# Start addresses of TensorE's operands at multiples of 256 bytes, and activations stored with all high parts ahead of all low parts

## The chip, the cores and the metric

The kernel runs on one core of a Trainium2 chip. The metric is the device time of one execution in microseconds (us), and a kernel's time is the median over its runs.

## The reference, cut to what matters

One layer of an encoder trunk on 256 tokens of width 1024, all in fp32:

```
x = x + 1/2 * SwiGLU_1(RMSNorm(x))                 # 1024 -> 2 x 2816 -> 1024
h = RMSNorm(x);  u = h @ W_in                      # 1024 -> 7904, split into parts
a = MLA(parts of u)                                # 16 heads of 96, 256 x 256 scores
m = BiSSD(parts of u)                              # conv, 32 heads, two scans, 2 chunks of 128
x = x + W_out( sigmoid(gA) * (a @ P_A) + sigmoid(gB) * (m @ P_B) )
x = x + 1/2 * SwiGLU_2(RMSNorm(x))
```

The weights are 124.5 MB, read once.

## The kernel before, in words

Activations lie transposed in SBUF: 128 features on the partitions (a "k tile"), 256 tokens along the free dimension. The weights stream through: `wload` (L112) fetches a piece of up to 1088 columns by one DMA on SP's queue, ScalarE writes its high part `whi` in the type fp32r, VectorE writes the rest `wlo = raw - whi`, and there are four buffers of each (raw, whi, wlo). An activation is split in the same way (`split`, L127) into a high part xh and a low part xl.

A product is three terms: whi·xh + whi·xl + wlo·xh. TensorE holds a 128 x 128 block of a weight still ("stationary", loaded by its own LDWEIGHTS ahead of each matmul) and streams 256 or 512 columns of the activation ("moving"). There are two forms of it:

- `wstat` (L135): three matmuls of 256 columns for each k tile, at L141, L142 and L143, into one accumulator. It serves W_in (`ps_in`), the second half of P_B (`ps_sb`), P_A (`ps_ab`) and W_out (`ps_o`, where the left operand is xs).
- `wstat2` (L145): a pair for each k tile, a matmul of 512 columns at L154 (whi against xh and xl, which lie side by side) and one of 256 at L153 (wlo against xh; the first of a chain is L156). It serves gate and up (`ps_gu`), down (`ps_d`), the gates gA and gB, and the first half of P_B (both `ps_half`).

The moving tiles are `xs` ([128, k, 2, 256]: for each k tile the high part and behind it the low part; two buffers in turn), `hs` (the hidden layer of 22 k tiles) and `ms` (the scan's output of 8 k tiles). In the attention's own projection (`ps_qkv`, L563 to L570) the roles are swapped: the weight moves, 192 or 256 columns, and a block of `cqh`, `cql`, `ckh` or `ckl` is stationary. Scores, transposes and the scan's last product are plain fp32 matmuls (`ps_sc`, `ps_pT`, `ps_xT`, `ps_cb`, `ps_y`).

The stages in order of time: gate and up of the first FFN (to 137 us of the span), down (to 200), W_in's first columns and first group (to 240), then attention heads, scan groups and the remaining columns of W_in interleaved by a table of keys (to 540), P_A, P_B and W_out (to 616), gate and up (to 733) and down of the second FFN. Within a stage the code's order sets each engine's order.

Where a tile starts in SBUF follows from the order in which pools are opened: one group grows from low addresses (`const`, `raw`, `w`, `x`, `xn`, `small`, then the stage's own pools), one from the high end (`pre` for W_in's first pieces, `ssd` for the scan). Addresses are per partition, in bytes; all are multiples of 32. What matters of them is the remainder by 256:

| tile | role on TensorE | start mod 256 before | after |
|---|---|---|---|
| whi, wlo (four buffers each) | stationary (moving in ps_qkv) | 32 | 0 |
| whi, wlo in pool pre | stationary in the first ps_in | 224 | 192 |
| xs (both buffers) | moving | 32 | 0 |
| hs | moving | 160 | 0 |
| ms | moving | 64 | 0 |
| cqh, cql, ckh, ckl | stationary | 160 | 0 |
| msk4 / eye / st1 | moving / stationary / moving (ps_pl) | 32 / 32 / 64 | 160 / 160 / 160 |
| cst (identity) | moving in transposes, fp32 | 0 | 128 |
| xz, xd, E | fp32 operands of the scan | 224 | 192 |
| qk, kv, pr | fp32 operands of attention | 192, 64, 64 | 32, 160, 160 |

A k tile, a block of a weight and a buffer are each a multiple of 256 bytes long, so a tile's remainder holds for all its slices.

Of the kernel before, what the change touches and what calls it, by code (L numbers as in the profile page):

```python
# [8 lines left out]
F32 = mybir.dt.float32  # L9
F32R = mybir.dt.float32r  # L10
# [5 lines left out]
P = 128  # L16
# [7 lines left out]

RAWB, WB = 4, 4
NMM, NPL, NG = 3, 2, 3
EB, PRB, QKB = 4, 2, 2
# [45 lines left out]
def build(ctx, tc, A, out, dbg=None):  # L73
# [6 lines left out]

    cp = ctx.enter_context(pool("const"))
    rawp = ctx.enter_context(pool("raw", RAWB))
    wp = ctx.enter_context(pool("w", WB))
    xp = ctx.enter_context(pool("x"))
    xnp = ctx.enter_context(pool("xn", 2))
    sm = ctx.enter_context(pool("small", 2))

    def dump(name, ap):
# [46 lines left out]
    def wstat(ps, pieces, xs, k0, first, last):  # L135

        ks = [(pc, j) for pc, j0, n in pieces for j in range(j0, j0 + n)]
        for i, (pc, j) in enumerate(ks):
            w = slice(j * P, (j + 1) * P)
            xh, xl = xs[:, k0 + i, 0], xs[:, k0 + i, 1]  # L140
            TE.matmul(ps, pc.hi[:, w], xh, start=first and i == 0, stop=False)  # L141
            TE.matmul(ps, pc.hi[:, w], xl, start=False, stop=False)  # L142
            TE.matmul(ps, pc.lo[:, w], xh, start=False, stop=last and i == len(ks) - 1)  # L143

    def wstat2(ps, pieces, xs, k0, first, last):  # L145


        ks = [(pc, j) for pc, j0, n in pieces for j in range(j0, j0 + n)]
        for i, (pc, j) in enumerate(ks):
            w = slice(j * P, (j + 1) * P)  # L150
            a, b = first and i == 0, last and i == len(ks) - 1
            if not a:
                TE.matmul(ps[:, 0], pc.lo[:, w], xs[:, k0 + i, 0], start=False, stop=False)  # L153
            TE.matmul(ps, pc.hi[:, w], xs[:, k0 + i], start=a, stop=b)  # L154
            if a:
                TE.matmul(ps[:, 0], pc.lo[:, w], xs[:, k0 + i, 0], start=False, stop=False)  # L156

# [53 lines left out]
    def xn_tiles():  # L211
        return xnp.tile([P, KD, 2, T], F32R, tag="xs", name="xs")

    class Norm:
# [12 lines left out]
        def scale(self, k):  # L227
            g = vec[:, self.vcol + k:self.vcol + k + 1]
            split(self.xs[:, k, 0], self.xs[:, k, 1], x[:, k], g)

# [15 lines left out]
    def ffn(norm, wgu, wd, after, hook=None):  # L246
        with ExitStack() as es:
# [3 lines left out]
            ps_r = es.enter_context(pool("ps_fr", 2, space=PSUM, reuse_waits="tile"))  # L251
            hs = hp.tile([P, KF, 2, T], F32R, name="hs")
            R = None
            for f in range(KF):
# [22 lines left out]
                tt(sg, sg, gu[:, 1], ALU.mult)  # L277
                split(hs[:, f, 0], hs[:, f, 1], sg)
            for d in range(KD):
# [97 lines left out]
    with ExitStack() as es:  # L377
# [9 lines left out]


        cqh = mp.tile([P, 3, T], F32R, name="cqh")
        cql = mp.tile([P, 3, T], F32R, name="cql")  # L390
# [18 lines left out]
        for k in range(KD):  # L409
            xr = m0.tile([P, T], F32, tag="xr", name="xr", bufs=2)  # L410
            stt(xr, x[:, k], vec[:, V_MIX + k:V_MIX + k + 1], R, ALU.mult, ALU.mult)
            split(xs[:, k, 0], xs[:, k, 1], xr)

# [93 lines left out]
        as_ = xn_tiles()  # L507
        ms = mp.tile([P, 8, 2, T], F32R, name="ms")
        mpb = mp.tile([P, 8, T], F32, name="mpb")

# [38 lines left out]
        def attn_group(g):  # L549
# [53 lines left out]
            def head(h):  # L603
# [31 lines left out]
                if h % 2:  # L635
# [7 lines left out]
                    i = g * HG // 2 + h // 2  # L643
                    split(as_[:, i, 0], as_[:, i, 1], po[:, :T])

# [3 lines left out]
        def ssd_group(g, xz):  # L649
# [57 lines left out]
            def finish():  # L707
# [10 lines left out]
                o = 4 * (g % 2)  # L718
                split(ms[:, o:o + 4, 0], ms[:, o:o + 4, 1], y)
                dump(f"m{g}", y)  # L720
# [63 lines left out]
        for c in range(4):  # L784
            branch(1, c)
            for d in range(2 * c, 2 * c + 2):
                tmp = mpb[:, d]
                tt(tmp, tmp, gt[4 + d // 2][:, d % 2], ALU.mult)
                tt(tmp, tmp, gt[d // 2][:, d % 2], ALU.add)
                split(os_[:, d, 0], os_[:, d, 1], tmp)  # L790
        dump("mg", mpb)
# [113 lines left out]
```

## Time and profile before

| | us |
|---|---|
| median of 3 runs | 811.11 |
| lowest, highest | 809.4, 811.33 |
| the profiled execution | 809.85 |
| its span, first to last instruction | 808.1 |
| TensorE busy in the span | 786.8 |
| VectorE, ScalarE busy | 625.0, 493.6 |

A matmul's row in the trace lasts from its start to the end of its results, and the next one starts while it still drains. So the busy time of TensorE counts drains too, and what a matmul costs in a row of them is the distance from its start to the next one's start, not its duration.

### The profile page before, as it was taken

Reading aid. Unit: us, or ns where it says so; the run is one execution under the profiler, and the core shown is the slowest. Engines: PE = TensorE matmul, PEld = TensorE weight load, DVE = VectorE, ACT = ScalarE, POOL = GpSimd, SP = SyncE. Lnnn points to the kernel's source line nnn. Section 1 sums busy time; section 2 is a strip of 40 time slices with the busy share of each in tenths; the row PEclk is TensorE's granted clock in tenths of the full one; section 3 lists DMA queues with packets and bytes.
Section 4 is the critical chain, followed back from the end, with each engine's and each line's share of the span. In section 5 each row is a group of like instructions: output and inputs, shape, how many; then the busy total and the mean of one; then the engine's idle time right before and its main releaser. Section 6 shows DMA issues by size and latency. Waiting matters only on the chain.

```text
span 808.1 us, 13739 instructions
## 1 busy us (share of the span) xinstructions
PE 786.8 (97%) x5232; PEld 700.4 (87%) x5232; DVE 625.0 (77%) x1276; ACT 493.6 (61%) x866; POOL 0.2 (0%) x4
## 2 busy tenths in 40 slices
PE   5999999999998999999999999999999999999998
PEld 4888888888998998988988887888998888888887
DVE  5899987667797986897898678767787877777553
ACT  6667665555367659569667675567455655655442
POOL 0000000000000000000000000000000000000000
PEclk9999999999999999999999999999999999999999
DMA  7667774667134443322325514441755465564772
GB/s 262 207 196 241 237 237 145 180 187 233 40 104 162 132 135 103 108 79 89 100 82 159 176 54 146 137 135 56 232 172 191 161 204 181 189 188 138 197 211 75
DMA packets 39090, 126.46 MB, mean 156 GB/s; under 512 B 4464, under 2 KB 5872, under 8 KB 39024
## 3 DMA queue, kind: packets, MB, share of 16 engines
q1 hardware_dynamic: 38592, 124.69, 48.6%
q10 hardware_dynamic: 432, 0.89, 0.3%
q8 instruction: 41, 0.67, 0.3%
q14 instruction: 25, 0.20, 0.1%
HBM read 124.52 MB, written 1.05 MB: 155 GB/s over the span
## 4 chain that ended last, share of the span: by engine, by line
PE 87%; DVE 6%; ACT 5%; issue 1%; DMA 1%; ACTq 0%
PE ps_gu L154 20%; PE ps_d L154 10%; PE ps_gu L153 9%; PE ps_half L154 5%; PE ps_d L153 5%; PE ps_in L142 4%; PE ps_in L143 4%; PE ps_in L141 4%; PE ps_y L700 3%; PE ps_half L153 2%; PE ps_sc L613 2%; PE ps_o L640 1%; PE ps_gu L156 1%; PE ps_pl L682 1%; DVE wlo L97 1%; PE ps_pT L630 1%
## 5 line engine op out<-in xcount | busy, mean ns | idle before, releaser
L97 DVE TENSOR_TENSOR wlo<-raw,whi 128x1024 fp32r<-128x1024 f32 (+4 forms) x256 | 289.1, 1131 | 75.5 <-ACT whi L94 74.6
L94 ACT ACTIVATE whi<-raw 128x1024 fp32r<-128x1024 f32 (+4 forms) x256 | 251.6, 986 | 145.4 <-PE ps_d L154 51.2
L154 PE MATMUL ps_gu<-xs,whi 128*128 128x512 f32 x704 | 243.8, 400 | 7.8 <-DVE xs L100 7.7
L153 PE MATMUL ps_gu<-xs,wlo 128*128 128x256 f32 x616 | 173.3, 281 | 1.8 <-DVE wlo L97 1.8
L154 PEld LDWEIGHTS ps_gu<-xs,whi 128*128 128x128 f32 x704 | 127.2, 190 | 32.2 <-ACT whi L94 7.2
L153 PEld LDWEIGHTS ps_gu<-xs,wlo 128*128 128x128 f32 x616 | 117.4, 191 | 6.4 <-DVE wlo L97 2.3
L154 PE MATMUL ps_d<-hs,whi 128*128 128x512 f32 x352 | 122.5, 393 | 0.0
L142 PE MATMUL ps_in<-xs,whi 128*128 128x256 f32 x368 | 105.3, 286 | 0.6 <-DVE xs L100 0.6
L143 PE MATMUL ps_in<-xs,wlo 128*128 128x256 f32 x368 | 105.0, 285 | 0.0
L141 PE MATMUL ps_in<-xs,whi 128*128 128x256 f32 x368 | 104.3, 283 | 0.0
L153 PE MATMUL ps_d<-hs,wlo 128*128 128x256 f32 x336 | 94.7, 282 | 0.0
L154 PEld LDWEIGHTS ps_d<-hs,whi 128*128 128x128 f32 x352 | 65.2, 188 | 13.8
L142 PEld LDWEIGHTS ps_in<-xs,whi 128*128 128x128 f32 x368 | 70.1, 190 | 1.2 <-DVE xs L100 0.8
L143 PEld LDWEIGHTS ps_in<-xs,wlo 128*128 128x128 f32 x368 | 70.1, 191 | 0.5 <-issue 0.3
L141 PEld LDWEIGHTS ps_in<-xs,whi 128*128 128x128 f32 x368 | 70.1, 190 | 0.1
L153 PEld LDWEIGHTS ps_d<-hs,wlo 128*128 128x128 f32 x336 | 63.1, 188 | 0.7
L94 ACT ACTIVATE gu<-ps_gu 128x512 f32<-128x512 f32 x44 | 26.1, 592 | 35.0 <-PE ps_gu L154 35.0
L100 DVE SCALAR_TENSOR_TENSOR xz<-ps_in,vec,xz 128x254 f32<-128x254 f32 (+1 forms) x96 | 44.7, 475 | 1.6 <-ACT xz L530 0.9
L154 PE MATMUL ps_half<-xs,whi 128*128 128x512 f32 x128 | 44.9, 399 | 0.0
L97 DVE TENSOR_TENSOR gu<-ps_gu,gu 128x512 f32<-128x512 f32 x44 | 30.3, 688 | 16.5 <-ACT gu L94 15.9
L97 DVE TENSOR_TENSOR E<-E,cb 128x512 f32<-128x512 f32 x48 | 32.0, 685 | 2.4 <-ACT E L691 1.5
L276 ACT ACTIVATE sg<-gu 128x256 f32<-128x256 f32 x44 | 18.1, 416 | 24.4 <-DVE gu L97 24.3
(232 smaller groups left out, 1375.5 us busy)
## 6 DMA issues: line engine op xcount, KB each, us to landing
raw<-in_w_gu SPq DMA_DIRECT2D x86, 512.0 KB, 3.9
raw<-in_w_in SPq DMA_DIRECT2D x62, 512.0 KB, 4.1
raw<-in_w_d SPq DMA_DIRECT2D x32, 384.0 KB, 3.2
raw<-in_w_d SPq DMA_DIRECT2D x32, 320.0 KB, 3.4
raw<-in_w_sb SPq DMA_DIRECT2D x16, 512.0 KB, 4.2
raw<-in_w_qkv SPq DMA_DIRECT2D x8, 544.0 KB, 3.8
raw<-in_w_ab SPq DMA_DIRECT2D x8, 512.0 KB, 3.8
raw<-in_w_o SPq DMA_DIRECT2D x8, 512.0 KB, 3.8
```

The source lines that it names most:

```text
L94: S.activation(dst, src, AF.Copy, scale=scale)
L97: V.tensor_tensor(out=dst, in0=a, in1=b, op=op)
L100: V.scalar_tensor_tensor(out=dst, in0=a, scalar=s, in1=b, op0=op0, op1=op1)
L141: TE.matmul(ps, pc.hi[:, w], xh, start=first and i == 0, stop=False)
L142: TE.matmul(ps, pc.hi[:, w], xl, start=False, stop=False)
L143: TE.matmul(ps, pc.lo[:, w], xh, start=False, stop=last and i == len(ks) - 1)
L153: TE.matmul(ps[:, 0], pc.lo[:, w], xs[:, k0 + i, 0], start=False, stop=False)
L154: TE.matmul(ps, pc.hi[:, w], xs[:, k0 + i], start=a, stop=b)
L156: TE.matmul(ps[:, 0], pc.lo[:, w], xs[:, k0 + i, 0], start=False, stop=False)
L276: S.activation(sg, gu[:, 0], AF.Silu)
L613: TE.matmul(sc[:, t * T:(t + 1) * T], qk[:HD, t * P:(t + 1) * P], qk[:HD, T:2 * T], start=True, stop=True)
L700: TE.matmul(py[64 * j:64 * j + 64, a:b], st[c, d][:, hh_], M[i][:, j, a:b], start=n == 0, stop=n == 3)
```

## The change

Three edits:

1. Pools are opened in another order and three pads (96, 120 and 8 words of 4 bytes) are put between them. The addresses become those of the table's last column.
2. xs, hs and ms go from [128, k, 2, 256] to [128, 2, k, 256]: the high parts of all k tiles, then the low parts of all. A slice of 256 columns stays one run. The 512 columns of L154 were one run of 2048 bytes; now they are two runs of 1024 bytes, 8 KB apart in xs and ms and 22 KB apart in hs.
3. ms and mpb are allocated ahead of the latent tiles instead of behind them.

Every instruction keeps its place on its engine, its waits and its element count; of the 5003 matmuls of the program not one is added, removed or moved. The only instructions that read or write in another shape are L154's matmuls and the split of ms in the scan (its four ScalarE and four VectorE instructions write one run of 1024 elements in place of four of 256).

```diff
+PAD0, PAD1, PAD2 = 96, 120, 8
-    cp = ctx.enter_context(pool("const"))
+    ctx.enter_context(pool("pad0")).tile([P, PAD0], F32, name="pad0")
     rawp = ctx.enter_context(pool("raw", RAWB))
     wp = ctx.enter_context(pool("w", WB))
     xp = ctx.enter_context(pool("x"))
     xnp = ctx.enter_context(pool("xn", 2))
+    cp = ctx.enter_context(pool("const"))
     sm = ctx.enter_context(pool("small", 2))
+    ctx.enter_context(pool("pad1")).tile([P, PAD1], F32, name="pad1")
+    ctx.enter_context(pool("pad2", side="right")).tile([P, PAD2], F32, name="pad2")
...
-            xh, xl = xs[:, k0 + i, 0], xs[:, k0 + i, 1]
+            xh, xl = xs[:, 0, k0 + i], xs[:, 1, k0 + i]
...
-            TE.matmul(ps, pc.hi[:, w], xs[:, k0 + i], start=a, stop=b)
+            TE.matmul(ps, pc.hi[:, w], xs[:, :, k0 + i], start=a, stop=b)
...
-        return xnp.tile([P, KD, 2, T], F32R, tag="xs", name="xs")
+        return xnp.tile([P, 2, KD, T], F32R, tag="xs", name="xs")
...
-            hs = hp.tile([P, KF, 2, T], F32R, name="hs")
+            hs = hp.tile([P, 2, KF, T], F32R, name="hs")
...
+        ms = mp.tile([P, 2, 8, T], F32R, name="ms")
+        mpb = mp.tile([P, 8, T], F32, name="mpb")
         cqh = mp.tile([P, 3, T], F32R, name="cqh")
...
-        ms = mp.tile([P, 8, 2, T], F32R, name="ms")
-        mpb = mp.tile([P, 8, T], F32, name="mpb")
...
-                split(ms[:, o:o + 4, 0], ms[:, o:o + 4, 1], y)
+                split(ms[:, 0, o:o + 4], ms[:, 1, o:o + 4], y)
```

## Rows read from the trace of the kernel before

**Rows 1.** The profile's page: busy time by engine, the clock that was granted in 40 slices of the span (in tenths), and the chain of work that ended last by engine.

```profile
PE 786.8 (97%) x5232; PEld 700.4 (87%) x5232; DVE 625.0 (77%) x1276; ACT 493.6 (61%) x866; POOL 0.2 (0%) x4
...
PEclk9999999999999999999999999999999999999999
...
PE 87%; DVE 6%; ACT 5%; issue 1%; DMA 1%; ACTq 0%
```

**Rows 2.** Busy time by stage: start and end of the stretch in us, its length, then for each engine the busy time and the number of instructions, the granted clock, the DMA engines' share and what they moved.

```profile
0.00:20.00 20.00, 10.93 (x42) 8.88 (x43) 12.09 (x34) 11.92 (x23) 0.20 (x4) 1.00 0.78 262
20.00:137.00 117.00, 116.72 (x669) 101.57 (x668) 102.74 (x172) 77.59 (x119) 0.00 (x0) 1.00 0.66 212
137.00:200.00 63.00, 63.00 (x365) 55.36 (x364) 41.27 (x66) 34.08 (x50) 0.00 (x0) 1.00 0.66 194
...
240.00:540.00 300.00, 293.62 (x2151) 260.73 (x2149) 243.86 (x588) 208.57 (x424) 0.00 (x0) 1.00 0.37 121
...
616.00:733.00 117.00, 116.40 (x668) 100.99 (x667) 92.76 (x141) 69.67 (x105) 0.00 (x0) 1.00 0.56 181
```

**Rows 3.** TensorE's matmuls grouped by line and shape over the whole span: count, then busy us and mean duration in ns.

```profile
L154 PE MATMUL ps_gu<-xs,whi 128*128 128x512 f32 x704 | 243.8, 400 | 7.8 <-DVE xs L100 7.7
...
L154 PE MATMUL ps_d<-hs,whi 128*128 128x512 f32 x352 | 122.5, 393 | 0.0
L142 PE MATMUL ps_in<-xs,whi 128*128 128x256 f32 x368 | 105.3, 286 | 0.6 <-DVE xs L100 0.6
...
L154 PE MATMUL ps_half<-xs,whi 128*128 128x512 f32 x128 | 44.9, 399 | 0.0
...
L154 PE MATMUL ps_half<-ms,whi 128*128 128x512 f32 x64 | 21.9, 393 | 0.0
L142 PE MATMUL ps_ab<-xs,whi 128*128 128x256 f32 x64 | 18.2, 286 | 0.0
```

**Rows 4.** TensorE in order of time in W_out, whose moving xs and stationary weights both start at 32: start in us, duration, the instruction. Nine matmuls of 256 columns lie from the first row to the last.

```profile
602.10 0.28 PE L141 MATMUL ps_o<-xs,whi 128*128 128x256 f32 x1
602.22 0.28 PE L142 MATMUL ps_o<-xs,whi 128*128 128x256 f32 x1
...
603.18 0.28 PE L141 MATMUL ps_o<-xs,whi 128*128 128x256 f32 x1
```

**Rows 5.** The same in the second half of P_B, where the moving ms starts at 64 and the weights at 32. Twelve matmuls from the first row to the last.

```profile
572.76 0.28 PE L141 MATMUL ps_sb<-ms,whi 128*128 128x256 f32 x1
572.88 0.28 PE L142 MATMUL ps_sb<-ms,whi 128*128 128x256 f32 x1
...
574.17 0.28 PE L141 MATMUL ps_sb<-ms,whi 128*128 128x256 f32 x1
```

**Rows 6.** The same in W_in's first columns, where the moving xs starts at 32 and the weights, in the pool pre, at 224. Twelve matmuls from the first row to the last.

```profile
206.09 0.28 PE L141 MATMUL ps_in<-xs,whi 128*128 128x256 f32 x1
206.20 0.28 PE L142 MATMUL ps_in<-xs,whi 128*128 128x256 f32 x1
...
207.50 0.28 PE L141 MATMUL ps_in<-xs,whi 128*128 128x256 f32 x1
```

**Rows 7.** The same in down, with the moving hs at 160 and the weights at 32: pairs of L154 (512 columns) and L153 (256). Nine pairs from the first row to the last.

```profile
161.76 0.39 PE L154 MATMUL ps_d<-hs,whi 128*128 128x512 f32 x1
161.99 0.28 PE L153 MATMUL ps_d<-hs,wlo 128*128 128x256 f32 x1
162.11 0.39 PE L154 MATMUL ps_d<-hs,whi 128*128 128x512 f32 x1
...
164.92 0.40 PE L154 MATMUL ps_d<-hs,whi 128*128 128x512 f32 x1
```

**Rows 8.** Single tiles' matmuls: count, then the shortest, median and longest duration in ns, and when the first and the last started. ps_sc and ps_cb are plain fp32 with 256 columns (moving qk at 192, xz at 224), ps_xT is plain fp32 with 128 columns (stationary xz at 224, moving identity at 0).

```profile
L154 PE MATMUL ps_d<-hs,whi x352: 387/396/400, 137.1 to 804.0; 128*128 128x512 f32 x176
L153 PE MATMUL ps_d<-hs,wlo x336: 274/282/286, 137.5 to 803.8; 128*128 128x256 f32 x168
...
L154 PE MATMUL ps_gu<-xs,whi x704: 387/395/766, 7.2 to 742.3; 128*128 128x512 f32 x176
L153 PE MATMUL ps_gu<-xs,wlo x616: 274/280/582, 8.3 to 742.2; 128*128 128x256 f32 x154
...
L141 PE MATMUL ps_o<-xs,whi x64: 282/283/386, 594.0 to 616.9; 128*128 128x256 f32 x64
...
L154 PE MATMUL ps_half<-ms,whi x64: 390/390/400, 419.8 to 454.4; 128*128 128x512 f32 x64
L153 PE MATMUL ps_half<-ms,wlo x56: 279/282/283, 432.6 to 454.3; 128*128 128x256 f32 x56
...
L613 PE MATMUL ps_sc<-qk x64: 377/379/484, 271.2 to 543.7; 96*128 96x256 f32 x64
...
L656 PE MATMUL ps_cb<-xz x16: 379/379/483, 253.3 to 494.2; 128*128 128x256 f32 x16
```

**Rows 9.** TensorE in order of time: seven plain fp32 transposes of 128 columns in one merged row, and ps_qkv's matmuls of 192 columns with a stationary block at 160; five of these lie from the second row to the third.

```profile
413.58 0.93 PE L664 MATMUL ps_xT<-cst,xz 128*128 128x128 f32 x7
...
425.11 0.28 PE L563 MATMUL ps_qkv<-whi,cqh 128*128 128x192 f32 x1
...
425.67 0.27 PE L565 MATMUL ps_qkv<-whi,cql 128*128 128x192 f32 x1
```

More of the change, by code (lines that the diff above doesn't have):

```diff
@@ L152, in wstat2 @@
             if not a:
-                TE.matmul(ps[:, 0], pc.lo[:, w], xs[:, k0 + i, 0], start=False, stop=False)
-            TE.matmul(ps, pc.hi[:, w], xs[:, k0 + i], start=a, stop=b)
+                TE.matmul(ps[:, 0], pc.lo[:, w], xs[:, 0, k0 + i], start=False, stop=False)
+            TE.matmul(ps, pc.hi[:, w], xs[:, :, k0 + i], start=a, stop=b)
             if a:
-                TE.matmul(ps[:, 0], pc.lo[:, w], xs[:, k0 + i, 0], start=False, stop=False)
+                TE.matmul(ps[:, 0], pc.lo[:, w], xs[:, 0, k0 + i], start=False, stop=False)
     def rsqrt(y, v, n):
@@ L228, in scale @@
             g = vec[:, self.vcol + k:self.vcol + k + 1]
-            split(self.xs[:, k, 0], self.xs[:, k, 1], x[:, k], g)
+            split(self.xs[:, 0, k], self.xs[:, 1, k], x[:, k], g)
         def square(self, k):
@@ L277, in ffn @@
                 tt(sg, sg, gu[:, 1], ALU.mult)
-                split(hs[:, f, 0], hs[:, f, 1], sg)
+                split(hs[:, 0, f], hs[:, 1, f], sg)
             for d in range(KD):
@@ L411, in build @@
             stt(xr, x[:, k], vec[:, V_MIX + k:V_MIX + k + 1], R, ALU.mult, ALU.mult)
-            split(xs[:, k, 0], xs[:, k, 1], xr)
+            split(xs[:, 0, k], xs[:, 1, k], xr)
         def latent(src, hi, lo, vcol, n):
@@ L643, in head @@
                     i = g * HG // 2 + h // 2
-                    split(as_[:, i, 0], as_[:, i, 1], po[:, :T])
+                    split(as_[:, 0, i], as_[:, 1, i], po[:, :T])
             return [proj] + [lambda h=h: head(h) for h in range(HG)]
@@ L789, in build @@
                 tt(tmp, tmp, gt[d // 2][:, d % 2], ALU.add)
-                split(os_[:, d, 0], os_[:, d, 1], tmp)
+                split(os_[:, 0, d], os_[:, 1, d], tmp)
         dump("mg", mpb)
```

## The prediction

> **What bounds the kernel now.** I read the page first, then the stages, then single matmuls in order of time. TensorE is busy 786.8 of 808.1 us, its clock is granted in full in every slice, and it carries 87% of the chain that ended last [rows 1]. By stage: in gate and up of both FFNs, in down and from 540 to 616 us TensorE never pauses, while VectorE, the next busiest, stands at 102.7 of 117 us at worst and the DMA engines at two thirds; in the interleaved stage from 240 to 540 us VectorE has 243.9 of 300 us and TensorE's pauses are short [rows 2]. So the kernel is as long as TensorE's stream of matmuls, and the change touches nothing but how fast that stream reads SBUF. The question is what a matmul costs beyond its columns, and how much of that hangs on addresses.
>
> The cost is the distance from start to start. In W_out nine matmuls of 256 columns take 1.08 us, 120 ns each [rows 4]; the row of such a matmul lasts 283 ns [rows 8], so in an unbroken stream distance is duration less 163 ns, and I use that to turn durations into distances. In down nine pairs take 3.16 us, 351 ns a pair [rows 7]; by the medians [rows 8] gate and up has (395 - 163) + (280 - 163) = 349. At the granted level, 2.4 GHz, one column a cycle would be 106.7 ns for 256 columns and 213.3 for 512, a pair 320. So a matmul in threes loses some 13 ns and a pair some 30: roughly a fixed loss for each matmul, not for each column (a loss by columns would be the same for 3 x 256 as for 512 + 256, and it is 40 against 30).
>
> Is that loss in every matmul? No. Plain fp32 streams at two cycles a column: seven transposes take 0.93 us, which is (930 - 273) / 6 = 109 ns each with 273 ns for the last one, the length that rows of their kind have [rows 9]; 256 columns take 379 - 163 = 216 [rows 8]. That is 2 to 3 ns over their columns, and that with operands at 224 and 192, off any round address. They load a new stationary block for each matmul too. So neither the load as such nor an odd address costs anything while the stream runs at half rate. The loss belongs to the full-rate fp32r stream, where an address can matter because there is no slack to hide a fetch.
>
> **The change part by part.**
>
> *Instructions:* none is added, removed or moved, and no wait changes. Cost nothing, and no queue is passed.
>
> *Start addresses of the weight matmuls.* What the trace has on addresses: moving at 64 instead of 32 gives (574.17 - 572.76) / 12 = 117.5 ns in place of 120 [rows 4, 5]; stationary at 224 instead of 32 gives (207.50 - 206.09) / 12 = 117.5 as well [rows 6]; for a pair, moving at 64 gives (390 - 163) + (282 - 163) = 346 against 349 to 351 [rows 7, 8]; 160 in place of 32 gives nothing [rows 7, 8]. So addresses do move the distance, by 2%, among values that are all off 128 bytes. No row has a full-rate stream at 0. I bound it. Below: nothing gained, or a little lost (rivals). Above: the fp32 rows' loss of about 2 ns, 109 for 256 columns and 216 for 512. Between them are the best matmuls of this very stream: the shortest rows of L153 last 274 ns and of L154 387 [rows 8], distances of 111 to 112 and 224, in gate and up as in down. These occur under the same instructions, so the stream can run at them; with the threes at 120 and pairs at 350 they are what is left when whatever collides does not. I take 112 and 224, a pair 336, because they are the nearest rows: same engine, same type, same load ahead of each matmul.
>
> Sum, with counts from the code and from the groups of matmuls [rows 3] (each pair has one L154; ps_in has 368 threes, of which 48 are of the pool pre at 117.5; ps_sb, ps_ab and ps_o have 64 threes each):
> - gate and up 704 pairs and down 352: 1056 x 14 ns = 14.8 us, in stages in which TensorE is the only bound. VectorE's 102.7 of 117 us would become 102.7 of about 112: still free.
> - ps_ab and ps_o, 384 matmuls x 8 = 3.1 us; ps_sb 192 x 5.5 = 1.1; ps_in of pre 144 x 5.5 = 0.8. Together 5.0 us, all of it on the path.
> - interleaved: gates and first half of P_B, 192 pairs x 13 = 2.5; the other 960 matmuls of ps_in x 8 = 7.7. Together 10.2 us, of which I count half: there heads and scan units hand over to ScalarE and VectorE and back, and a wait whose end they set is not shortened by a faster product before it.
> - sum 14.8 + 5.0 + 5.1 = 24.9 us.
>
> *Two runs in place of one for the 512 columns.* No row shows a moving operand in two runs. If the second run starts like a stream that goes on, it costs nothing; if it starts like a matmul of its own, the 512 cost two distances of 256. At the forecast's own rate that is 2 x 112 = 224, the same. At today's rate it is 2 x 120 = 240 against 230 to 233, some 8 ns. I take nothing here; the 8 ns are the slower rival.
>
> *Other tiles that move.* Attention's fp32 operands go from multiples of 64 to 32 or 160, the scan's from 224 to 192, the identity from 0 to 128. The fp32 rows show no loss at 224 and 192 [rows 8], so nothing. The ps_pl matmuls move from 32 and 64 to 160; 2.5 ns on half of 192 is 0.2 us, left out. ScalarE, VectorE and the DMAs write to other addresses; if one of them slows by a few per cent, the spare time of VectorE in rows 2 covers it in all stages but gate and up, where 9 us of 112 would be left.
>
> The profiled execution is 809.85 us with a span of 808.1, 1.3 us under the median. Span 808.1 - 24.9 = 783.2, execution 785, and against the median 811.1 - 24.9 = 786.2. I say 786.
>
> **The rivals.**
>
> *All of the loss goes.* Distances of 109 and 216, a pair 325: FFN pairs 1056 x 25 = 26.4; ps_ab and ps_o 384 x 11 = 4.2; ps_sb and pre 336 x 8.5 = 2.9; half of the interleaved 192 x 23 + 960 x 11 = 15.0 is 7.5. Sum 41 us: 770. For it: the fp32 rows lose only that much. Against it: five matmuls of ps_qkv with 192 columns at full rate take 0.56 us, 112 ns each for 80 ns of columns [rows 9], so the next block's load sets a floor of 110 or more beside a full-rate stream, unless the load is itself slowed by its start at 160. The Trainium skill's page "TensorE: Matmul & The Clock Gate", section "Back-to-back issue gap", gives N / 2.4 + 2.5 ns when warm, 109.2 and 215.8: by it this rival is the outcome. The fp32 rows agree with its 2.5 ns, the fp32r rows of 120 and 233 do not.
>
> *Addresses aren't the cause.* The load of the next block reads SBUF beside a full-rate stream and takes some 13 ns from it wherever both start; or what counts is how the two starts lie to each other. For it: moving and stationary both at 32 is the slowest case (120), and 64 against 32 or 32 against 224 are the faster ones [rows 4 to 6], and after the change both are at 0, equal again. Then the FFNs, ps_in, ps_ab and ps_o stay, and ps_sb's 192 matmuls go back to 120, 0.5 us lost: 811 to 812. Against it: the shortest rows, 274 and 387, stand in tiles with both at 32 [rows 8]. A page speaks for the same result: the Trainium skill's "SBUF — State Buffer", section "Specifications (TRN2)", has lines of 16 bytes, of which all addresses here are multiples already, so by it 256 brings nothing. That 64 and 32 differ in rows 4 and 5 is not what such lines would do.
>
> *Only what 64 and 224 show.* 3 ns on 1056 pairs, 2.5 on the 384 matmuls of ps_ab and ps_o and on half of the 960 of ps_in: 3.2 + 1.0 + 1.2 = 5.4 us, 806.
>
> *Slower: the second run starts anew.* The place is L154, 1248 times; the price 8 ns, if the addresses gain nothing. 1056 x 8 = 8.4 us in the FFNs and up to 1.5 in the rest: 820. It decides as soon as a run's start costs more than the addresses give back to a pair. For it: the loss of today is one for each start of a stream. Against it: it is as well one for each load, and a second run has no load.
>
> **How the numbers follow.** Forecast 0.38 (786), all of the loss 0.15 (770), only a little 0.10 (806), addresses not the cause 0.20 (811), slower 0.17 (820). A measurement of this kernel can tell about 0.3%, 2.4 us, from no change. Faster: 0.38 + 0.15 + 0.10 = 0.63; within 0.3%: 0.20; slower: 0.17. For 8 in 10 I leave out most of the slower rival above and the lower end of the full recovery below: 767 to 815. The likeliest case alone, with none or all of the interleaved part counted: 781 to 791.
>
> **What would show it.** Right: L153 with a median duration near 275 in place of 280 to 282 and L154 near 387 in place of 395; ps_o and ps_ab near 275 in place of 283; gate and up and down shorter by 4% each; VectorE's busy time unchanged, its share of gate and up risen. All of the loss: medians of 272 and 379. Not the cause: 283 everywhere, ps_sb risen from 280 to 283. Slower: L154 at 400 or more, with L153 and the threes as before. The forecast is wrong if the shortest rows of today are short because their neighbour is long, that is if 112 is paid back by the 512 beside it; and its size is wrong if VectorE in gate and up or the hand-overs from 240 to 540 us take the gain.

## The result and the profile after

The change left the time almost where it was, a little above: 811.04 us in the median of 20 runs (809.73 to 811.97) beside 809.73 in 20 runs of the kernel before (808.43 to 811.35). The ratio is 1.0014, with an interval of 1.0008 to 1.002. The forecast was 786. It and its rivals were reckoned from 811.11, the median of 3 runs of before, which is 1.4 us more than that of 20.

The page of the kernel after, the lines that answer to [rows 1]: busy time by engine, the granted clock in 40 slices, the chain that ended last.

```profile
PE 788.1 (97%) x5232; PEld 700.5 (87%) x5232; DVE 625.8 (77%) x1276; ACT 494.0 (61%) x866; POOL 0.2 (0%) x4
...
PEclk9999999999999999999999999999999999999999
...
PE 86%; DVE 6%; ACT 5%; issue 1%; DMA 1%; ACTq 0%
```

Nothing has taken TensorE's place. With the same 5232 matmul records in the trace it is busy 1.3 us longer than before, at the same clock, and the profiled execution (811.15 us, span 809.4) is 1.3 us longer than that of before. VectorE and ScalarE are within 0.8 us of what they had, so writing to other addresses cost them next to nothing.

Single tiles of the kernel after (count; shortest, median and longest duration in ns; first and last start in us), ps_d in two stretches, first FFN and second:

```profile
L160 PE MATMUL ps_gu<-xs,whi x704: 387/395/767, 7.1 to 743.3; 128*128 128x512 f32 x176
L159 PE MATMUL ps_gu<-xs,wlo x616: 274/280/583, 8.2 to 743.1; 128*128 128x256 f32 x154
...
L160 PE MATMUL ps_d<-hs,whi x176: 389/398/403, 137.1 to 198.9; 128*128 128x512 f32 x176
L159 PE MATMUL ps_d<-hs,wlo x168: 274/281/284, 137.5 to 198.8; 128*128 128x256 f32 x168
...
L160 PE MATMUL ps_d<-hs,whi x176: 389/398/403, 743.5 to 805.3; 128*128 128x512 f32 x176
...
L147 PE MATMUL ps_sb<-ms,whi x64: 283/283/283, 571.8 to 594.5; 128*128 128x256 f32 x64
...
L147 PE MATMUL ps_o<-xs,whi x64: 282/283/385, 594.9 to 617.8; 128*128 128x256 f32 x64
```

The same tiles before, of those that moved:

```profile
L154 PE MATMUL ps_d<-hs,whi x176: 387/396/400, 137.1 to 198.6; 128*128 128x512 f32 x176
...
L154 PE MATMUL ps_d<-hs,whi x176: 387/396/400, 742.5 to 804.0; 128*128 128x512 f32 x176
...
L141 PE MATMUL ps_sb<-ms,whi x64: 280/280/284, 571.3 to 593.6; 128*128 128x256 f32 x64
```

Beside [rows 8], gate and up and ps_o have not moved by a nanosecond in the median (395, 280, 283). ps_sb rose from 280 to 283, which is the mark that the prediction named for "addresses aren't the cause". And down became slower: from the first to the last start of L160 lie 198.9 - 137.1 = 61.8 us over 175 pairs, 353.1 ns a pair, and 61.8 again in the second FFN. In the trace of before both stretches are 61.5 long, 351.4 a pair. Down thus gave up 0.6 us and ps_sb 192 x 2.2 = 0.4; the rest of the 1.3 us is spread over the other stages at 0.2 or less.

### The profile page after: what moved, and what is told of

Same layout as the page of the kernel before. It is cut to its first block, busy times and chain, and to the rows that moved or that the text cites. A ratio compares the mean times of both kernels' runs of the same rounds, so it can differ in the third digit from the quotient of the medians.

```text
span 809.4 us, 13739 instructions
## 1 busy us (share of the span) xinstructions
PE 788.1 (97%) x5232; PEld 700.5 (87%) x5232; DVE 625.8 (77%) x1276; ACT 494.0 (61%) x866; POOL 0.2 (0%) x4
## 4 chain that ended last, share of the span: by engine, by line
PE 86%; DVE 6%; ACT 5%; issue 1%; DMA 1%; ACTq 0%
PE ps_gu L160 20%; PE ps_d L160 10%; PE ps_gu L159 9%; PE ps_half L160 5%; PE ps_d L159 5%; PE ps_in L148 4%; PE ps_in L149 4%; PE ps_in L147 4%; PE ps_y L706 3%; PE ps_half L159 2%; PE ps_sc L619 2%; PE ps_o L646 1%; PE ps_gu L162 1%; PE ps_pl L688 1%; DVE wlo L103 1%
## 5 line engine op out<-in xcount | busy, mean ns | idle before, releaser
L160 PE MATMUL ps_gu<-xs,whi 128*128 128x512 f32 x704 | 244.3, 400 | 7.7 <-DVE xs L106 7.6
L160 PEld LDWEIGHTS ps_gu<-xs,whi 128*128 128x128 f32 x704 | 127.5, 190 | 32.3 <-ACT whi L100 7.1
L160 PE MATMUL ps_d<-hs,whi 128*128 128x512 f32 x352 | 123.2, 398 | 0.0
L160 PEld LDWEIGHTS ps_d<-hs,whi 128*128 128x128 f32 x352 | 65.2, 188 | 14.8
L160 PE MATMUL ps_half<-xs,whi 128*128 128x512 f32 x128 | 45.0, 400 | 0.0
L159 PE MATMUL ps_half<-xs,wlo 128*128 128x256 f32 x112 | 32.0, 285 | 0.0
```

The lines of the kernel that those rows point to most:

```text
L159: TE.matmul(ps[:, 0], pc.lo[:, w], xs[:, 0, k0 + i], start=False, stop=False)
L160: TE.matmul(ps, pc.hi[:, w], xs[:, :, k0 + i], start=a, stop=b)
```

## The experiments

Distances below are from one matmul's start to the next one's. Where no row is shown they are means over a stage, worked out from the starts in the trace. Every kernel but e1 is the kernel after with an edit. e1 to e4 ran beside a median of before of 809.29 us, e5 to e7 beside 809.49, e8 to e11 beside 809.26, e12 beside 809.24.

The theories at the outset: the change failed because one part took back what the other gave (the two runs against the addresses); because it is the difference between the two starts that counts, and not the remainder of each; because the load of the next block takes the time; or because the moving stream loses it by itself, wherever it starts.

### The two parts apart: e1 and e2

e1 has the new tiles in the pools of before, e2 the old tiles in the new pools.

```diff
# e1, against the kernel before
-        return xnp.tile([P, KD, 2, T], F32R, tag="xs", name="xs")
+        return xnp.tile([P, 2, KD, T], F32R, tag="xs", name="xs")
...
# e2, against the kernel after
-        return xnp.tile([P, 2, KD, T], F32R, tag="xs", name="xs")
+        return xnp.tile([P, KD, 2, T], F32R, tag="xs", name="xs")
...
```

> The layout alone: xs, hs and ms as [128, 2, k, 256], so that the 512 columns are two runs, with the pools and so all remainders by 256 as before (weights and xs 32, hs 160, ms 64). Theory S (what slows a full-rate matmul is that its moving operand and the stationary block that is loaded beside it start at the same remainder): nothing changes; a pair of down stays at 350 ns, a matmul of ps_sb at 117.5 (rows 280), time within 0.1% of before. Rival R (a second run costs a new start, and that is what made down slower): pairs of down at 353 (L154 rows up by 3 ns), gate and up as well, time 0.15% or more above before. Rival L (each load takes a fixed 13 ns from a full-rate stream, addresses matter little): nothing changes, as S.

> The start addresses alone: the pools and pads of the changed kernel, so weights, xs, hs and ms all at 0, but each k tile's low part right behind its high part, 512 columns in one run. S: down at 353 ns a pair and ps_sb at 120 a matmul, as with both edits, since the two now start alike; the first ps_in (weights at 192) at 113.5; time 0.1 to 0.2% above before. R: down back at 350, time as before. L: down and ps_sb as before within 1 ns.

e1 took 809.3 us (ratio 1.0001, 0.9992 to 1.001), e2 810.98 (1.0017, 1.0008 to 1.0026). Down of the first FFN and ps_sb, of e1:

```profile
L154 PE MATMUL ps_d<-hs,whi x176: 387/396/400, 136.6 to 198.0; 128*128 128x512 f32 x176
...
L141 PE MATMUL ps_sb<-ms,whi x64: 280/280/284, 570.8 to 593.0; 128*128 128x256 f32 x64
```

The same of e2:

```profile
L160 PE MATMUL ps_d<-hs,whi x176: 389/398/403, 135.7 to 197.5; 128*128 128x512 f32 x176
...
L147 PE MATMUL ps_sb<-ms,whi x64: 283/283/283, 570.4 to 593.1; 128*128 128x256 f32 x64
```

With two runs and old addresses both rows are as before; with one run and new addresses both are as after, to the shortest and longest duration. Two runs cost nothing that shows, and the addresses alone bring the whole of the 0.14%. Nothing was gained that something else took back.

### The tiles that lost: e9

hs goes back to a remainder of 160 and ms to 64, the rest stays at 0.

```diff
+MOFF, HO = 16, [40, 40]        # words
-            hs = hp.tile([P, 2, KF, T], F32R, name="hs")
+            hs = hp.tile([P, 2 * KF * T + 64], F32R, name="hs")
+            hs = hs[:, ho:ho + 2 * KF * T].rearrange("p (a k t) -> p a k t", a=2, k=KF)
... (ms likewise)
```

> The changed kernel with only hs and ms put back to the remainders of before, 160 and 64, while weights and xs stay at 0: down's moving operand then lies 160 from the weights (128 before), ms 64 (32 before). If the changed kernel's 0.14% come from down and ps_sb, whose operands it brought to equal starts, both recover: down from 351 to 349 or 350 a pair, ps_sb from 120 to 118, and the time goes back to that of before, within 0.1%. If they come from elsewhere (other tiles' addresses, ScalarE, VectorE, DMA): 0.1 to 0.2% above before, as the changed kernel.

808.91 us, ratio 0.9996 (0.9988 to 1.0005): the time of before. Its down (first FFN) and ps_sb:

```profile
L163 PE MATMUL ps_d<-hs,whi x176: 389/392/400, 137.1 to 198.0; 128*128 128x512 f32 x176
...
L150 PE MATMUL ps_sb<-ms,whi x64: 280/280/283, 571.9 to 594.1; 128*128 128x256 f32 x64
```

ps_sb is back at 280, and a pair of down takes 60.9 / 175 = 348 ns, less than the 351 of before, where the weights start at 32. So hs at 160 has no fixed price of its own: with the weights at 0 in place of 32 it is 3 ns a pair cheaper.

### Does the difference of the starts set the distance? e3, e4, e5

e3 puts two pads of 32 words around the weights' pool, so that weights start at 128 and moving tiles at 0. e4 and e5 give each moving tile an offset of its own, with the weights at 0 (192 in the first ps_in).

```diff
# e3
+    ctx.enter_context(pool("padw")).tile([P, 32], F32, name="padw")
     wp = ctx.enter_context(pool("w", WB))
+    ctx.enter_context(pool("padx")).tile([P, 32], F32, name="padx")
# e4: bytes / 4 of the six xs tiles in order of time, ms, hs of both FFNs
+XO = [32, 48, 32, 16, 48, 16]
+MOFF, HO = 8, [32, 16]
# e5
+XO = [48, 32, 48, 48, 56, 24]
+MOFF, HO = 48, [48, 8]
```

> The changed kernel with a pad of 128 bytes ahead of the pool of whi and wlo and one of 128 behind it: the weights start at 128 by 256, every moving operand at 0. S: no weight matmul but the first ps_in has equal starts any more: threes at 114 or less in place of 120 (rows 277 in place of 283), pairs at 345 or less in place of 350 to 353; 576 threes' matmuls of ps_ab, ps_sb and ps_o save 3 us, the FFNs 1056 pairs x 5 to 8 = 5 to 8 us, the interleaved stage 2 to 4; time 797 to 802. L: rows of 281 to 283, time 809 to 812. If what counts is the start by 128 alone, as in lines of 128 bytes, nothing changes either, since 0 and 128 are then alike: 811.

> The changed kernel with the weights at 0 and each moving tile at a remainder of its own: gate and up of the first FFN 128, the first ps_in 192 (its weights are at 192 too), ps_in of the groups and the gates 128, ps_ab 64, ps_o 192, ms 32, down of the first FFN 128, gate and up and down of the second 64. S: the first ps_in goes from 113.5 to 120 ns (rows 276 to 283), and ps_ab, ps_sb, ps_o and the other ps_in go from 120 to 118 or less; which offset is best, S doesn't say. L: 117 to 120 everywhere, no order by offset. Time by S 800 to 808, by L 810 to 812.

> The changed kernel with the weights at 0 and other remainders of the moving tiles: 192 for gate and up and down of the first FFN, for ps_in of the groups, the gates, ps_ab and ms; 128 for the first ps_in, whose weights are at 192, so that it lies 192 behind them by 256; 224 for ps_o; 96 for gate and up and 32 for down of the second FFN. The sweep before gave 113.3 ns a matmul in ps_o at 192 against 120 at 0, and 117.7 to 120 at 32, 64 and 128. Theory C (the load of the next stationary block and the full-rate stream read SBUF side by side and get in each other's way; how often depends on how far one starts from the other, by 256): 113 to 114 at 192 wherever threes run, the first ps_in too; that saves 6.5 ns x 384 in ps_ab and ps_sb and some of 6 ns x 960 in ps_in, so 3 to 8 us against the changed kernel, 803 to 808. Rival T (113 in ps_o was that tile's or that stage's own): ps_ab, ps_sb and ps_in stay at 118 to 120. For pairs C has no number ahead of the run; up to now every offset gave 349 to 351.

e3 took 809.67 us (1.0006, 0.9995 to 1.0017) and is far from the 797 to 802 that theory S forecast; e4 808.62 (0.9985, 0.9975 to 0.9995), between the forecasts of S and L; e5 807.7 (0.9974, 0.9963 to 0.9984), within theory C's 803 to 808, though its 113 to 114 at 192 came in W_in alone and P_A and ps_sb stayed at 118. W_out of e4 (moving at 192, weights at 0):

```profile
L150 PE MATMUL ps_o<-xs,whi x64: 276/276/386, 594.1 to 615.9; 128*128 128x256 f32 x64
```

The second half of P_B of e5, with the same 192 and 0:

```profile
L150 PE MATMUL ps_sb<-ms,whi x64: 281/281/281, 569.7 to 592.0; 128*128 128x256 f32 x64
```

All that was seen, by the difference of moving less stationary start, mod 256:

| difference | matmuls in threes, ns (median duration less 163) | a pair of down, ns (first to last start / 175) |
|---|---|---|
| 0 | 120 (ps_sb and ps_o of after, first ps_in of e4) | 353 (after) |
| 32 | 117 (ps_sb of before), 120 (ps_sb of e4) | 348 (e5, second FFN) |
| 64 | 116 (ps_ab of e4), 113 (first ps_in of after), 116 (that of before and of e2) | 352 (e4, second FFN) |
| 128 | 118 (ps_o of e3), 120 (ps_sb of e3, by its starts) | 351 (before), 351 (e3), 352 (e4, first FFN) |
| 160 | | 348 (e9) |
| 192 | 113 (ps_o of e4), 118 (ps_sb of e5) | 353 (e5, first FFN) |
| 224 | 118 (ps_o of e5) | |

Threes of true operands with equal starts ran at 120 in every case, whether both are at 32, at 0 or at 192, and nothing was slower. Other differences give 113 to 120, and the same difference gives 113 in one stage and 118 in another, or 117 and 120 (32). Pairs stay within 348 to 353 whatever the starts, those of gate and up within 349 to 352; at equal starts gate and up takes 350, down 353. So the start addresses do act, but the difference alone does not settle the rate, and all that they move is the 7 ns between 113 and 120 in the threes and 5 of a pair, not the 30 that a pair loses.

That addresses alone do not fix the rate shows in the first ps_in too. After (moving at 0, weights at 192):

```profile
L148 PE MATMUL ps_in<-xs,whi x55: 276/276/467, 199.2 to 222.0; 128*128 128x256 f32 x55
```

e2, with the same starts:

```profile
L148 PE MATMUL ps_in<-xs,whi x55: 276/279/468, 198.8 to 221.6; 128*128 128x256 f32 x55
```

### Is it the load? e6 and e7

In e6 the stationary block has fewer columns in the middle of each chain: 64 of 128 in gate, up and P_A, 32 in down and W_out. The rest of those products is left out, so fewer rows of the result are written too. In e7 the whole block is loaded, but from one address per partition (gate, up, down, P_A, W_out and the second half of P_B).

```diff
# e6, L141 and the like
-            TE.matmul(ps, pc.hi[:, w], xl, start=False, stop=False)
+            TE.matmul(ps[:n], pc.hi[:, v], xl, start=False, stop=False)   # v: n of the 128 columns
# e7
+            if bw:
+                wh, wl = (t[:, j * P:j * P + 1].to_broadcast([P, P]) for t in (pc.hi, pc.lo))
```

> The changed kernel, all weight operands and moving tiles at 0, with narrower stationary blocks in the middle of each chain: 64 of 128 columns in gate and up and in ps_ab, 32 in down and in ps_o; ps_in, ps_sb and ps_half keep 128. The rest of those products is left out, the moving columns and the number of matmuls stay. Theory C: the loss shrinks with the length of the load: threes at 113 with 64 and 110 with 32 columns in place of 120, pairs at 335 and 328 in place of 350. Rival F (each full-rate matmul loses a fixed time at its own start, whatever is loaded): 120 and 350 as before. ps_sb, unchanged, stays at 120 in both.

> The changed kernel with a stationary block that repeats its first column 128 times (a broadcast, so the load reads one word per partition again and again) in gate and up, down, ps_ab, ps_sb and ps_o; ps_in and ps_half keep true blocks. It computes another product there. Number and length of loads and of matmuls stay. Theory C: the load walks through no lines of its own, so the meetings change: if one line is fetched once, threes go to 109 to 112 and pairs to 325 to 335. F: 120 and 350. If it is the length of the load as an instruction and not its reads that counts: 120 and 350 too, and then e6 tells the two apart.

One execution each: e6 801.73 us, e7 806.91. Gate and up of the second FFN and down of the first in e6:

```profile
L163 PE MATMUL ps_gu<-xs,whi x352: 387/388/584, 612.3 to 735.4; 128*64 128x512 f32 x132, 128*128 128x512 f32 x44
L162 PE MATMUL ps_gu<-xs,wlo x308: 274/274/285, 612.6 to 735.2; 128*64 128x256 f32 x154
...
L163 PE MATMUL ps_d<-hs,whi x176: 388/392/396, 133.8 to 194.0; 128*32 128x512 f32 x160, 128*128 128x512 f32 x16
```

and in e7:

```profile
L166 PE MATMUL ps_d<-hs,whi x176: 388/396/398, 137.2 to 198.1; 128*128 128x512 f32 x176
```

A quarter of the load takes a pair of down from 353 to 60.2 / 175 = 344 ns, a load from one address to 60.9 / 175 = 348. In gate and up half of the load takes a pair from 350 to 344, a load from one address to 347. So the load has a share of the loss, 2 to 9 ns of the 30 to 33 over the 320 of the columns, and not the rest; half of it brings a pair to the same 344 as a quarter, so the price does not simply go with the load's length, and neither theory C (335 and 328) nor rival F (350) came out. That e6 writes fewer rows of the result could have a part in its gain; e7 writes them all. The threes agree: with one address P_A, P_B's second half and W_out run at 117, 117 and 114 ns in place of 120, in e6 P_A (64 columns) at 115 and W_out (32) at 117.

The first two rows of e6 show one thing more. Their medians, 388 and 274, are the ones that the prediction named as the sign of success, and by its rule of duration less 163 they would make a pair of 336. The starts give 344. The medians of two kinds of matmul that alternate in a pattern need not add up to its period.

### Is it the stream itself? e8 and e12

In e8 the moving operand reads its first column again and again: in gate, up and P_A with the true load, in down and W_out with the load of e7 as well. e12 repeats a short run instead of one word: 16 words in gate and up of the first FFN and P_A, 8 in down of the first, 4 in ps_sb, 64 in gate and up of the second and W_out, 32 in down of the second.

```diff
# e8
+            if bm:
+                xh, xx = xh[:, 0:1].to_broadcast([P, T]), xx[:, :, 0:1].to_broadcast([P, 2, T])
# e12
+            if r:
+                xh = xh[:, 0:r].unsqueeze(1).to_broadcast([P, T // r, r])
+                xx = xx[:, 0, 0:r].unsqueeze(1).to_broadcast([P, 2 * T // r, r])
```

> The changed kernel with a moving operand that repeats its first column (one word per partition read again and again) in gate and up and in ps_ab, with moving operand and stationary block both so in down and in ps_o, and with neither in ps_sb, ps_in and ps_half. It computes other products there; number, length and order of matmuls and loads stay. With loads of a half and a quarter of the columns pairs went from 349 to 342 and not on to 328, so that theory C explains only part of the loss. Theory C2 (the rest is the stream's own reading of SBUF): with one address pairs of gate and up at 320 to 335 and threes of ps_ab at 107 to 111; with both at one address still less, 320 to 328 and 107 to 110. Rival I (the rest, 113 for 256 columns and 228 for 512, lies in TensorE or in its results, not in SBUF): ps_ab not under 113 and gate and up not under 340, down and ps_o the same.

e8, one execution: 785.93 us, 23.3 less than before beside it. Gate and up, down of the first FFN, P_A and ps_sb (left as in after):

```profile
L171 PE MATMUL ps_gu<-xs,whi x704: 377/381/764, 7.3 to 722.4; 128*128 128x512 f32 x176
L170 PE MATMUL ps_gu<-xs,wlo x616: 271/271/583, 8.3 to 722.3; 128*128 128x256 f32 x154
...
L171 PE MATMUL ps_d<-hs,whi x176: 377/381/383, 130.1 to 187.5; 128*128 128x512 f32 x176
...
L152 PE MATMUL ps_ab<-xs,whi x64: 272/275/460, 526.1 to 559.3; 128*128 128x256 f32 x64
...
L152 PE MATMUL ps_sb<-ms,whi x64: 283/283/283, 559.6 to 582.3; 128*128 128x256 f32 x64
```

Gate and up goes to 381 and 271 in the median; the means of its distances are 219 and 109 ns, a pair of 328, with every block still loaded in full. Down, whose load reads one address too, has 57.4 / 175 = 328: the same. So a stream that stays at one address loses about 8 ns a pair over its columns with either load; the rest of the loss comes with the stream's own walk through SBUF, and a load was seen to cost something only beside a stream that walks. Rival I is out; theory C2 has its figures, but not the further gain that it expected from down.

> The changed kernel with a moving operand that repeats its first few words: 4 words (16 bytes) in ps_sb, 8 words in down and 16 words (64 bytes) in gate and up of the first FFN, 16 words in ps_ab, 32 words (128 bytes) in down and 64 words (256 bytes) in gate and up of the second, 64 words in ps_o. It computes other products there; columns, loads and order stay. One word repeated gave 327 ns a pair and 111.6 a matmul in ps_ab, true operands 349 to 351 and 120. Theory W (a stream is slowed by walking through ever new addresses, whatever lies in them): short repeats cost as one word does, up to the length at which a fetch ends, and the true figure from there. Rival M (it is slowed by what it asks of the memory each cycle, whichever word it is, and one word alone is served from a register): already 4 or 8 words cost as the true operand, 349 and 120. Where the step lies isn't forecast: by W somewhere from 64 to 256 bytes, by M ahead of 16 bytes.

e12, one execution: 809.88 us. Gate and up of the first FFN (16 words) and of the second (64), down of the first (8) and of the second (32), ps_sb (4):

```profile
L166 PE MATMUL ps_gu<-xs,whi x352: 394/407/766, 7.2 to 141.9; 128*128 128x512 f32 x176
L165 PE MATMUL ps_gu<-xs,wlo x308: 277/284/579, 8.2 to 141.8; 128*128 128x256 f32 x154
...
L166 PE MATMUL ps_gu<-xs,whi x352: 387/395/579, 617.7 to 741.7; 128*128 128x512 f32 x176
...
L166 PE MATMUL ps_d<-hs,whi x176: 377/381/383, 142.1 to 199.7; 128*128 128x512 f32 x176
...
L166 PE MATMUL ps_d<-hs,whi x176: 397/397/402, 741.9 to 804.0; 128*128 128x512 f32 x176
...
L149 PE MATMUL ps_sb<-ms,whi x64: 272/275/275, 573.0 to 594.1; 128*128 128x256 f32 x64
```

Repeating 16 bytes (ps_sb, 275 - 163 = 112 ns) or 32 bytes (57.6 / 175 = 329 a pair) costs what one address costs. At 64 bytes a pair takes (407 - 163) + (284 - 163) = 365, more than the 350 of the true operand; at 128 bytes 62.1 / 175 = 355, beside 353 for down's true operand; at 256 bytes gate and up of the second FFN has the true operand's means, 234 and 116. So the loss sets in between 32 and 64 bytes (no length between was run), and no start address can spare it: a run of 1024 bytes is sixteen times 64 wherever it starts. Nor is it that fewer different words are read: 16 words over and over cost more than all of them. That is theory W, with the step earlier than it put it and an excess at 64 bytes that it does not have; rival M is out.

### A version from what was seen: e10 and e11

e10 keeps pairs and threes and gives each moving tile the offset that was best in e4 and e5: 0 in gate and up, 192 in W_in, the gates, P_A, W_out and ms, 128 in the first ps_in, 32 in hs. e11 puts all of them at 192 (128 in the first ps_in) and makes every pair three matmuls of 256 into one accumulator, so that adding the halves falls away; it computes the same.

```diff
# e10
+XO = [0, 32, 48, 48, 48, 0]
+MOFF, HO = 48, [8, 8]
# e11
+XO = [48, 32, 48, 48, 48, 48]
+MOFF, HO = 48, [48, 48]
-                    wstat2(ps, [(pcs[0], 0, 6), (pcs[1], 0, 5)], hs, 11 * c, c == 0, c == 1)
+                    wstat(ps[:, 0], [(pcs[0], 0, 6), (pcs[1], 0, 5)], hs, 11 * c, c == 0, c == 1)
... (gate and up, the gates and P_B likewise)
```

> The changed kernel with the remainder that was best so far for each use, the weights at 0: xs at 0 in gate and up of both FFNs, 192 in ps_in of the groups, the gates, ps_ab and ps_o; 192 from its weights in the first ps_in; ms 192, hs 32. From the two sweeps: ps_in 115, ps_ab and ps_sb 116 to 118, ps_o 113.5, gate and up 349, down 347 a pair: against the sweep with 807.7 us gate and up gain 1 us, down 1, ps_o 0.8, so 804 to 806; 0.4 to 0.6% under before. If the threes' rate is settled by how a stream happens to fall in step and not by the offset, 806 to 809.

> All moving tiles at 192 and the weights at 0 (the first ps_in 192 behind its weights), and every product in threes of 256 columns into one accumulator in place of pairs of 512 and 256 into two, so that the copy and the sum of two halves in gate and up, down, gates and the first half of P_B fall away too. It computes the same. By C a three at 113.5 is 340 ns where a pair is 349, for 1248 of them up to 11 us, and at 117.5 it is 353, 4 us lost; ps_in at 192 had both. So 798 to 811, the middle 804; by rival I as well, since that is the same floor by columns.

e10 took 804.84 us (803.6 to 806.42 in 5 runs), ratio 0.9946 (0.9934 to 0.9958): half a per cent below before, within the 804 to 806 that was forecast, and the best steady version here. Its down has 390 and 282 in the median and takes 348 ns a pair by the starts; W_in beyond the first columns runs at 276, 113 ns in the median, instead of 283; its ps_o came out at 281 this time, where e4 had 276 with the same starts.

e11 has 807.27 in the median, but its 12 runs lie between 799.06 and 815.08, a spread that no other kernel here has; no ratio is given for that reason. Its profiled execution (808.68) shows a likely reason: down of the first FFN and, behind it, of the second (as far as 800 us):

```profile
L150 PE MATMUL ps_d<-hs,whi x176: 276/276/276, 139.3 to 198.8; 128*128 128x256 f32 x176
...
L150 PE MATMUL ps_d<-hs,whi x167: 281/281/281, 741.2 to 799.8; 128*128 128x256 f32 x167
```

The same instructions at the same remainders run at 113 ns all through the first FFN's down and at 118 all through the second's, without one in between. Gate and up goes with it: 113 in the first FFN, 118 in the second. One FFN's 1584 matmuls by 4.5 ns are 7.1 us. The 12 runs lie in three groups of four, 799 to 801, 805.5 to 808.7 and 813 to 815 us, some 7 us apart, and the profiled one, with one FFN at either rate, is of the middle group. That is what two, one or no FFN at the faster rate would give; that the outer groups are so was not seen, since only one execution was traced.

### The two rates seen matmul by matmul

The distances in ns, one behind the other, worked out from the starts in the traces; a pair is written 512 + 256:

```
before, gate and up, one chain     233+117 231+112 233+117 231+113
before, gate and up, another       241+120 236+113 233+117
before, down                       234+120 224+122 234+120 233+120 225+121
after, down, first chain           233+117 231+112 233+117 231+113
after, down, the other chains      241+120 236+113 233+117 241+120 236+113 233+117
e10, down                          228+119 228+118 229+118 228+119 228+118
after, ps_sb                       120 120 120 120 120 120
e11, down of the first FFN         113 114 113 113 114 113
e11, down of the second FFN        117 118 118 118 117 118 118 117 119
e8, gate and up                    219+108 220+108 219+109
```

The stream settles into a pattern that repeats, to within a nanosecond or two, until the chain of accumulation ends. Two pairs as in the first line are 693 ns, 346.5 a pair; three as in the second are 1060, 353.3. In the down of after, the first chain of each FFN runs in the first pattern (346.6 over its 20 whole pairs) and the other seven in the second (353.6); in e2, with the same addresses, the first chain of the second FFN fell into the second pattern as well. Before, all sixteen chains of down ran alike, at 350.4, in a pattern between the two, and in e10 all at 347.3. That is where down's 0.6 us come from: 14 of 16 chains went from the middle pattern to the slow one, and two to the fast one.

## Why the prediction was wrong

*That the kernel is as long as TensorE's stream, and that nothing else would become late:* right. TensorE's busy time and the span rose by the same 1.3 us, and in e8, where the shorter distances of pairs and threes add up to about 27 us, the span is 25.3 us under that of after (784.1 and 809.4).

*That instructions, two runs and the other tiles that move cost nothing:* right. e1 shows it for the two runs (ratio 1.0001), with which the slower rival, 8 ns at L154, is dead. L160 does come near that rival's 400 ns in down (398), but does so with one run in e2 as well.

*That neither the load as such nor an odd address costs anything at half rate, so that the loss belongs to the full-rate stream:* right as far as it goes. The fp32 rows of ps_sc and ps_cb stay at 379 with the other addresses of after, and by e8 most of the full-rate stream's loss goes with its walk. From there the prediction went to "where an address can matter", and took the start for the address. What costs time is the walk past 32 bytes, and the start takes none of it away. Nor is there a floor of 110 from the load, as the prediction read from ps_qkv: in e8 256 columns take 108 to 109 with every block loaded in full.

*That pairs go to 112 and 224:* this is the step that failed. The shortest rows of L153 and of L154 were added up as if they could stand side by side. In the trace of before the 224 of down stand beside 122, and the 112 of gate and up beside 231 to 233: a short matmul is one beat of a pattern, and no pair of true operands in these lists takes less than 343, which the next one of the pattern makes up. e6 shows it once more, with medians of 388 and 274 and a pair of 344. The prediction names this as what would make it wrong ("if 112 is paid back by the 512 beside it"), and the answer stood in the same trace, in the starts of [rows 7] in full. With 336 a pair the 1056 pairs of the FFNs carried 14.8 us of the sum; measured, they lost 0.6. The 112 was carried over to the threes as well, though the shortest row of ps_o was 282: ps_ab and ps_o, put down for 8 ns a matmul, gave nothing, and ps_sb lost 2.2 ns a matmul.

*The rival "addresses aren't the cause", 811 to 812, chance 0.20,* is what happened: FFN gate and up, ps_in, ps_ab and ps_o stay, ps_sb falls back to 120. Its argument that equal starts at 0 are as slow as equal starts at 32 holds in every stage of threes; that the rate hangs on "how the two starts lie to each other" holds for equal starts, and for others only in part. Its 811 to 812 lies so near to 811.04 by some luck: it was 0.5 us on top of 811.11, where before stands at 809.73, and it had no term for down, which pays more than ps_sb. Its load, "some 13 ns from it wherever both start", is only part: e6 gives back 6 to 9 ns of a pair, not 26.

*All of the loss goes (325 a pair):* nearly that rate exists, 328 in e8, but for a stream that doesn't walk. The Trainium skill's page "TensorE: Matmul & The Clock Gate", section "Back-to-back issue gap", gives N / 2.4 + 2.5 ns for a matmul by itself when warm, an estimate of 109.2 for 256 columns and 215.8 for 512; 108 to 109 and 219 in e8 come near it, 112 to 122 and 224 to 241 of true operands do not.

What stays open: why a walking stream loses some 20 ns a pair, why a repeat of 64 bytes is worse than a long run, and what decides at a chain's start which of two patterns the stream falls into. No run here separates these. Only remainders by 256 were varied on purpose; whether a tile's place beyond that counts is not known.

## What to carry to other kernels

Neither the shortest durations of a distribution nor its median need be a rate at which the stream can run: before a forecast rests on them, write the distances of neighbours one behind the other and add up a whole period. To learn whether an operand's reading costs time, let it read one address over and over and look at the distance; that bounds what any layout or alignment could bring before one is built. Of start addresses, equal starts of moving and stationary were never better than 120 ns for a three, others gave 113 to 120 without a rule that the difference alone would give; trying two or three offsets for each tile brought 0.5% here, while rounding them all to 256 bytes brought equal starts.

## What the runs showed of the hardware that was not expected

- Matmuls of full-rate fp32r in an unbroken chain run in repeating patterns, and within one execution the same instructions at the same remainders can run in either of two: 113 or 118 ns for 256 columns (e11), 346.5 or 353.3 for a pair (down of after).
- A moving operand that stays within 16 or 32 bytes costs 109 to 112 ns for 256 columns (e12); one that repeats 64 bytes costs 121 in gate and up and 123 in P_A, more than the 116 and 120 of the true operand there. The Trainium skill's page "SBUF — State Buffer", section "Specifications (TRN2)", has lines of 16 bytes and a penalty at each crossing; in e12 a repeat of 32 bytes, which crosses one, costs what one address costs, and the step lies between 32 and 64 bytes.
- A weight load slows a walking fp32r stream: a pair of 353 ns becomes 344 with a quarter of the load, and 348 with a whole load from one address (e7). The Trainium skill's page "TensorE: Matmul & The Clock Gate", section "Step-by-step: what each phase is for", gives the load a read port of its own that takes nothing from the running matmul; e8 agrees for a stream at one address, e6 and e7 do not for a true one.
